# The second experts' shared expert: from fp32 products to products of split operands

## The chip, the cores and the metric

The kernel runs on one core of one Trainium2 chip. Its metric is the device time of one execution in microseconds; the median of three runs before the change is 1669.13 us (1666.88 to 1670.62). The engines are TensorE (PE), VectorE (DVE), ScalarE (ACT), GpSimd (POOL) and SyncE (SP), which issues most transfers.

## The reference

Two transformer blocks on 512 rows of 1024 columns. The first has a sparse attention beside a gated linear attention, then 32 experts, 2 for each row. The second has latent attention (MLA) beside attention with forget gates, and then these experts:

```python
h = rms_norm(x, g_ffn_norm) * (1 + scale_f) + shift_f
scores = sigmoid(h @ w_router)                 # 64 experts in 8 groups
choice = scores + b_router                     # 4 groups are kept, of these the 6 best experts
gate = scores[chosen] / sum(scores[chosen]) * 2.5
routed = sum over chosen e of gate_e * ((silu(h @ Wg[e]) * (h @ Wu[e])) @ Wd[e])
shared = (silu(h @ w_sh_gate) * (h @ w_sh_up)) @ w_sh_down     # 1024 -> 256 -> 1024, for all rows
x = x + gate_f * (shared + routed)
out = rms_norm(x, g_final)
```

All inputs and outputs are fp32. An fp32 product on PE is two passes, which the trace records as two instructions. The projections of both mixers avoid it: a matrix is split into a high part in fp32r (a format that PE takes in one pass) and the low part that is left, and three products (high by high, high by low, low by high) are summed in PSUM. This is `k.mm3` (lines 106 to 113).

## The kernel before, in words

Phases follow each other: mixer 1, 32 experts, mixer 2 (`phase_c`), 64 experts (`phase_d`, `rest_d`). Between phases, work overlaps where buffers and queues allow it. Rows are in four tiles (t = 0 to 3) of 128; `xres` is the residual in SBUF.

*Output projection wo* (`finish` in `phase_c`, L1805 to 1829). For each of two column groups of 512, four PSUM banks (one for each t) take eight steps of k, three products each: 96 matmuls of 128x512. The weights come by SP in four pieces of 256x512 (L130); ACT makes the high part wh (L136), DVE the low part wl (L137). DVE then multiplies a bank by the gate row gm (L1824, `wo<-wo,gmr`) and adds it to xres (L1825), and the bank is free for the second group. After the second group's add of tile t, `done(t)` starts the norm of that tile.

*Head of the second experts.* `head` and `logits` (L1886 to 1911): sum of squares on ACT, the root on DVE and ACT, then two steps on DVE: h = xres * rs * gs, and the shift, h + sh (L1903); h goes to DRAM (hD), is transposed on PE (xt, L1908), copied by ACT to hT, and multiplied with the router's weights (lg, L1911). `rest_d` starts with the sigmoid on ACT (L1931), adds the bias (L1933, `cv<-cv,br`), and follows a chain of small DVE steps that picks the experts up to Ab, the 0/1 matrix of choices (L1974). From Ab come, by small PE products and DVE steps, the counts cnt, the ranks of the experts (perm), the positions pos, posT and posR, the gates GT and Gr, and by bc and st the list ii of a unit's rows (L915).

*Shared expert.* Between these stand its products: gate and up g and u (L975) in fp32 with 128x256 outputs, hid = silu(g) * u (L977, L979), transposes (L986), y (L999), the scaling by the row gf on DVE into `ysh` (L1007), and the add to xres on POOL (L1993). Its weights sg (gate, up) and sd (down) come by `load_from` (L816 to 826).

*Units.* The routed experts run in 33 units of 128 rows, each of one or two experts' rows. For a unit, POOL gathers rows of hD by an indirect DMA into xg (L917), PE transposes them (L940), and multiplies with wg, wu (L975) and wd (L999); a product with a 0/1 matrix puts the result back to rows (L1053), and DVE adds it to xres.

*What sets the order.* A scheduler orders instructions on each engine by priorities (`high_priority`) when the program is built; an engine takes them in that order. Weights live in slots of 8 KB a partition, which `moe.slot` hands out from three pools (15, 2 and 1 slots) by the tables O1, then O2; a slot's next load waits for the last use of what it held. `rows`, `gmr` (the gate row gm, the norm's gain, later the router's weights), h4, hT4, sg and sd take slots as well. `moe.fetch(n)` loads the weights of units below n; F0 and F1 say up to which unit before and within the router. Experts from the fifth on are read through perm, by a register that SP loads (TENSOR_LOAD).

Of the kernel before, what the change touches and what calls it, by code (L numbers as in the profile page):

```python
# [7 lines left out]
F32 = mybir.dt.float32  # L8
F32R = mybir.dt.float32r
# [3 lines left out]
AF = mybir.ActivationFunctionType  # L13
# [5 lines left out]
S, D = 512, 1024  # L19
NT = 4  # L20
KD = 8
# [646 lines left out]
WS = (0, 1, 2, 2, 3, 3)  # L668
LAST = 2


# [76 lines left out]
class Moe:  # L748
# [33 lines left out]
    def slot(self, shape, dt, name, hold=False, after=None):  # L782


        t = self.W[next(self.order)].tile(shape, dt, tag="w8", name=name)
        if hold or after is not None:
            corner = t[:, 0, :1] if len(shape) == 3 else t[:, 0, 0, :1]
            with ExitStack() as c:
                if after is not None:
                    c.enter_context(self.k.tc.issue_after(after))  # L790
                self.k.nc.gpsimd.memset(corner, 0.0)
        return t

    def load(self, es, after=None, spread=(), free=0):
# [21 lines left out]
        return [(x[:2], x[2]) for x in g]  # L816

    def load_from(self, wg, wu, wd):

        nc = self.k.nc  # L820
        g = [self.slot([128, KD, 256], F32, "sg") for _ in range(2)]
        for t, w in zip(g, (wg, wu)):
            nc.sync.dma_start(t, w.rearrange("(p k) f -> p k f", p=128))
        d = self.slot([128, 2, D], F32, "sd")
        nc.sync.dma_start(d, wd.rearrange("(p j) n -> p j n", p=128))
        return g, d

# [229 lines left out]
    def run(self):  # L1057
        n = len(self.units)
        for u in range(2):
            self.pick(u)  # L1060
        self.prep(0)
        with self.k.tc.issue_after(self.indexed.ins):
            self.prep(1)
        if self.E == 32:
# [766 lines left out]

F0, F1 = 2, 3
NS = 9
RM = 15
RW = 1
O1 = [0] * 3 + [1] * 2 + [0] * 12
O2 = [0] * 3 + [1] * 2 + [2] + [0] * 12
LP = 300
RP = 300
FL = 0  # L1840
# [3 lines left out]
def phase_d(k, out):  # L1844
    nc, tc, I = k.nc, k.tc, k.I
    E = 64
    ctx = ExitStack()
# [12 lines left out]
    f = ctx.enter_context(tc.tile_pool(name="pd", bufs=1, reuse_waits="tile"))  # L1860
    moe_consts(k, f)
    gf = row(k, f, k.modD[5 * D:], "gf")
    moe.scale = gf
    perm = f.tile([1, E], I32, name="perm")
    rows_ = moe.slot([128, 2, D], F32, "rows")
    sh, gs = rows_[:, 0], rows_[:, 1]
# [12 lines left out]
    hTs = [hT4[t // 2][:, t % 2] for t in range(NT)]  # L1879
    shared = moe.load_from(I["w_sh_gate_2"][0], I["w_sh_up_2"][0], I["w_sh_down_2"][0])  # L1880
    moe.fetch(F0, 0)
    lbs = []
# [15 lines left out]
    def logits(t):  # L1898
# [3 lines left out]
        nc.vector.scalar_tensor_tensor(h, k.xres[:, t], rs, gs, op0=ALU.mult, op1=ALU.mult)  # L1902
        nc.vector.tensor_add(h, h, sh)  # L1903
        nc.scalar.dma_start(moe.hD[ts], h)
# [8 lines left out]
    def rest():  # L1913
        for t in range(NT - LL, NT):
            with tc.high_priority(LP):
                logits(t)
        moe.rooms()
        moe.work()
        rest_d(k, out, moe, lbs[0], br, f, perm, hTs, shared, ctx)
    return gm, head, rest  # L1920


def rest_d(k, out, moe, lb, br, f, perm, hTs, shared, ctx):
    nc, tc, I = k.nc, k.tc, k.I
# [60 lines left out]

    ws = [(128, shared)]
    hTx = moe.m.tile([128, NT, 2, 128], F32, tag="xT", name="hTx", bufs=1)
    for t in range(NT):
        moe.hidden(hTs[t], ws, None, k.pbank, hT=hTx[:, t])
    for t in range(NT):  # L1990
        def add(h, b):
            xs = k.xres[:, t, h * 512:(h + 1) * 512]
            nc.gpsimd.tensor_add(xs, xs, moe.scaled(h, b, moe.m.tile([128, 512], F32, tag="yl", name="ysh", bufs=2)))  # L1993
        moe.down(hTx[:, t], ws, add)
    moe.run()
# [72 lines left out]
```

## Time and profile before

| | us |
|---|---|
| median of 3 runs | 1669.13 |
| lowest, highest | 1666.88, 1670.62 |
| profiled execution | 1662.47 |
| its span | 1660.7 |
| PE busy in it | 1540.4 (93%) |
| DVE, ACT, POOL busy | 962.3, 542.9, 331.5 |

The profiled execution is 6.7 us under the median. A time in the trace is counted from the span's start. In a timeline row stand start, duration, engine, line, operation, output <- input, shape, the count of merged instructions, and in brackets the idle time of the engine ahead of it with what ended it. In a row of stages stand the busy time of each engine, PE's granted clock as a share of full speed, the DMA engines' mean share, and GB/s. A matmul's recorded duration is longer than its turn, since matmuls overlap; the distance of starts gives the rate.

### The profile page before, as it was taken

Reading aid. Unit: us, or ns where it says so; the run is one execution under the profiler, and the core shown is the slowest. Engines: PE = TensorE matmul, PEld = TensorE weight load, DVE = VectorE, ACT = ScalarE, POOL = GpSimd, SP = SyncE. Lnnn points to the kernel's source line nnn. Section 1 sums busy time; section 2 is a strip of 40 time slices with the busy share of each in tenths; the row PEclk is TensorE's granted clock in tenths of the full one; section 3 lists DMA queues with packets and bytes.
Section 4 is the critical chain, followed back from the end, with each engine's and each line's share of the span. In section 5 each row is a group of like instructions: output and inputs, shape, how many; then the busy total and the mean of one; then the engine's idle time right before and its main releaser. Section 6 shows DMA issues by size and latency. Waiting matters only on the chain.

```text
span 1660.7 us, 28614 instructions
## 1 busy us (share of the span) xinstructions
PE 1540.4 (93%) x10917; PEld 1037.9 (62%) x10917; DVE 962.3 (58%) x2188; ACT 542.9 (33%) x1100; POOL 331.5 (20%) x281
## 2 busy tenths in 40 slices
PE   5899999978998878899999998999999999999996
PEld 5665557765565547675657776865666665565663
DVE  3598636854564346547554635555665666666656
ACT  4534776331111125555552222301211211112112
POOL 2323541012111102230104442022101101111000
PEclk9999999988999998899999999999999999999998
DMA  6443326368999963233006836849999999999961
GB/s 189 148 164 112 114 80 242 126 216 323 418 416 416 419 256 105 73 93 103 26 1 191 263 111 233 308 184 366 375 414 388 398 416 417 423 419 420 420 287 64
DMA packets 104783, 420.78 MB, mean 253 GB/s; under 512 B 23508, under 2 KB 30138, under 8 KB 67268
## 3 DMA queue, kind: packets, MB, share of 16 engines
q1 hardware_dynamic: 82880, 388.20, 60.7%
q0 software_dynamic: 9968, 19.04, 3.2%
q10 hardware_dynamic: 11796, 11.68, 2.1%
q8 instruction: 87, 1.43, 0.3%
q14 instruction: 52, 0.43, 0.1%
HBM read 419.99 MB, written 9.21 MB: 258 GB/s over the span
## 4 chain that ended last, share of the span: by engine, by line
PE 49%; DVE 6%; DMA 4%; POOL 1%; ACT 1%; issue 1%; SPq 0%; DVEq 0%; ACTq 0%; POOLq 0%
PE g L975 8%; PE u L975 8%; PE sc L1053 7%; PE y L999 7%; PE qk L1690 2%; DMA mw<-in_w_mod_dram 2%; PE pt L110 2%; PE pt L108 2%; PE pt L109 2%; PE ob L1718 2%; PE xT L940 2%; PE pt L1710 1%; DVE macc L1402 1%; PE pr L109 1%; PE pr L108 1%
## 5 line engine op out<-in xcount | busy, mean ns | idle before, releaser
L137 POOL TENSOR_TENSOR wl<-w,wh 128x1024 fp32r<-128x1024 f32 (+4 forms) x68 | 156.6, 2305 | 360.4 <-ACT wh L136 336.9
L1054 DVE TENSOR_TENSOR xres<-xres,sc 128x512 f32<-128x512 f32 x368 | 224.3, 679 | 3.5 <-PE sc L1053 1.0
L975 PE MATMUL u<-wu,xT 128*32 128x256 f32 (+2 forms) x2240 | 175.3, 386 | 11.2 <-DMA wu<-in_w_exp_up_dram 9.4
L975 PE MATMUL g<-wg,xT 128*32 128x256 f32 (+2 forms) x2240 | 172.9, 382 | 3.1 <-DMA wg<-in_w_exp_gate_dram 3.1
L999 PE MATMUL y<-wd,hT 128*32 128x512 f32 (+2 forms) x1120 | 167.6, 596 | 0.0
L917 POOL DMA_INDIRECT xg<-hD,ii x46 | 46.1, 1002 | 597.1 <-issue 499.8
L981 DVE SCALAR_TENSOR_TENSOR hid<-u,gc,hid 128x256 f32<-128x256 f32 x46 | 22.2, 484 | 234.3 <-PE u L975 234.3
L975 PEld LDWEIGHTS g<-wg,xT 128*32 128x32 f32 (+2 forms) x2240 | 98.9, 118 | 89.6 <-issue 31.0
L1053 PE MATMUL sc<-yh,st 128*128 128x512 f32 x368 | 152.1, 416 | 0.0
L136 ACT ACTIVATE wh<-w 128x1024 fp32r<-128x1024 f32 (+4 forms) x88 | 89.9, 1021 | 185.1 <-PE pt L109 71.6
L975 PEld LDWEIGHTS u<-wu,xT 128*32 128x32 f32 (+2 forms) x2240 | 104.3, 120 | 73.2 <-DMA wu<-in_w_exp_up_dram 12.2
L1053 PE MATMUL sc<-yl,st 128*128 128x512 f32 x368 | 144.4, 395 | 0.1
L989 ACT ACTIVATE hT<-hT 128x256 f32<-128x256 f32 x46 | 17.7, 385 | 298.8 <-PE hT L986 298.8
L116 ACT ACTIVATE yh<-y 128x512 fp32r<-128x512 f32 x92 | 55.0, 597 | 163.3 <-DVE y L1007 129.4
L108 PE MATMUL pr<-wh,xh 128*128 128x512 f32 (+2 forms) x256 | 102.1, 403 | 5.9 <-ACT wh L136 5.4
L109 PE MATMUL pr<-wl,xh 128*128 128x512 f32 (+2 forms) x256 | 101.8, 399 | 5.9 <-POOL wl L137 5.9
L999 PEld LDWEIGHTS y<-wd,hT 128*32 128x32 f32 (+2 forms) x1120 | 46.6, 118 | 90.7 <-issue 88.6
L117 DVE TENSOR_TENSOR yl<-y,yh 128x512 fp32r<-128x512 f32 x92 | 63.6, 691 | 67.1 <-ACT yh L116 66.7
L110 PE MATMUL pr<-wh,xl 128*128 128x512 f32 (+2 forms) x256 | 100.3, 396 | 0.2 <-DVE xl L117 0.2
L110 PE MATMUL pt<-xh,wl 128*128 128x512 f32 x224 | 89.2, 398 | 1.8 <-POOL wl L137 1.7
L108 PE MATMUL pt<-xh,wh 128*128 128x512 f32 x224 | 89.8, 401 | 0.1
L109 PE MATMUL pt<-xl,wh 128*128 128x512 f32 x224 | 88.6, 396 | 0.0
(540 smaller groups left out, 2797.7 us busy)
## 6 DMA issues: line engine op xcount, KB each, us to landing
wg<-in_w_exp_gate_dram SPq DMA_DIRECT2D x96, 1024.0 KB, 12.7
wu<-in_w_exp_up_dram SPq DMA_DIRECT2D x96, 1024.0 KB, 12.4
wd<-in_w_exp_down_dram SPq DMA_DIRECT2D x96, 1024.0 KB, 11.5
w<-in_w_in_dram SPq DMA_DIRECT2D x52, 512.0 KB, 3.8
mw<-in_w_mod_dram SPq DMA_DIRECT2D x32, 512.0 KB, 6.0
mw<-in_w_mod_dram SPq DMA_DIRECT2D x8, 1024.0 KB, 6.0
w<-in_w_out_dram SPq DMA_DIRECT2D x16, 512.0 KB, 4.9
brs<-brd ACTq DMA_DIRECT2D x1, 2560.0 KB
```

The lines of the kernel that those rows point to most:

```text
L108: nc.tensor.matmul(out, lhsT=lh, rhs=rh, start=first, stop=False)
L109: nc.tensor.matmul(out, lhsT=lh, rhs=rl, start=False, stop=False)
L110: nc.tensor.matmul(out, lhsT=ll, rhs=rh, start=False, stop=last)
L116: hi = nc.scalar.activation(dh, src, AF.Copy)
L117: lo = nc.vector.tensor_sub(dl, src, dh.bitcast(F32))
L136: nc.scalar.activation(wh[:, :, :c], w[:, :, :c], AF.Copy)
L137: (eng or nc.gpsimd).tensor_sub(wl[:, :, :c], w[:, :, :c], wh[:, :, :c].bitcast(F32))
L917: self.gathered = nc.gpsimd.indirect_dma_start(out=x, out_offset=None, in_=src, in_offset=bass.IndirectOffsetOnAxis(ap=ii[:, :1], axis=0), ...
L975: nc.tensor.matmul(b[sl], lhsT=xT[:, kk, sl], rhs=g[h][:, kk], start=kk == 0, stop=kk == KD - 1)
L999: nc.tensor.matmul(b[sl], lhsT=hT[:, j, sl], rhs=d[:, j, h * 512:(h + 1) * 512], start=j == 0, stop=j == 1)
L1053: nc.tensor.matmul(b, lhsT=st[:, ts], rhs=y[h][i], start=i == 0, stop=i == 1)
L1054: nc.vector.tensor_add(self.acc[:, t, hs], self.acc[:, t, hs], b)
```

## The change

The shared expert is computed from split operands. Its gate and up weights stand side by side in two tiles sgu of 512 columns, which are split into sgh (ACT) and sgl (DVE); sd is multiplied by gf once and split into sdh and sdl; hT is split into hh (ACT) and hl (DVE), the latter behind the last tile's shift (`shifted[-1]`). `gu(t)` makes gate and up of a tile in one bank by 24 products of 128x512, `turned(t)` the hidden rows, their transposes and their split into mh and mid; y then comes scaled, and DVE adds it from PSUM to xres. The tables O1 and O2, F0 and the priorities of the first units' preparation are new as well.

```diff
@@ -667,6 +667,7 @@
 OB = [1] * 4 + [0] * 7 + [1] + [2] * 2 + [3] * 3
 WS = (0, 1, 2, 2, 3, 3)
 LAST = 2
+RUN = {32: 0, 64: 400}
 
 
 SEQ = "mfmtmtmfmtmtmmtmmtmtmmtmmtmtmtm"
@@ -788,7 +789,7 @@
             with ExitStack() as c:
                 if after is not None:
                     c.enter_context(self.k.tc.issue_after(after))
-                self.k.nc.gpsimd.memset(corner, 0.0)
+                self.k.nc.gpsimd.memset(corner.bitcast(F32) if dt == F32R else corner, 0.0)
         return t
 
     def load(self, es, after=None, spread=(), free=0):
@@ -814,16 +815,6 @@
             g[i][2] = self.slot([128, 2, D], F32, "wd", after=after)
             self.last.append(get(g[i][2], sl(self.wd, e)))
         return [(x[:2], x[2]) for x in g]
-
-    def load_from(self, wg, wu, wd):
-
-        nc = self.k.nc
-        g = [self.slot([128, KD, 256], F32, "sg") for _ in range(2)]
-        for t, w in zip(g, (wg, wu)):
-            nc.sync.dma_start(t, w.rearrange("(p k) f -> p k f", p=128))
-        d = self.slot([128, 2, D], F32, "sd")
-        nc.sync.dma_start(d, wd.rearrange("(p j) n -> p j n", p=128))
-        return g, d
 
     def rank(self, m, perm):
 
@@ -1056,11 +1047,12 @@
 
     def run(self):
         n = len(self.units)
-        for u in range(2):
-            self.pick(u)
-        self.prep(0)
-        with self.k.tc.issue_after(self.indexed.ins):
-            self.prep(1)
+        with self.k.tc.high_priority(RUN[self.E]):
+            for u in range(2):
+                self.pick(u)
+            self.prep(0)
+            with self.k.tc.issue_after(self.indexed.ins):
+                self.prep(1)
         if self.E == 32:
             self.fetch(3, after=self.gathered.ins, free=NF)
         self.take(0)
@@ -1829,13 +1821,14 @@
     return finish
 
 
-F0, F1 = 2, 3
+F0, F1 = 1, 3
 NS = 9
 RM = 15
 RW = 1
-O1 = [0] * 3 + [1] * 2 + [0] * 12
-O2 = [0] * 3 + [1] * 2 + [2] + [0] * 12
+O1 = [0] * 18 + [1] * 2 + [0] * 6
+O2 = [0, 2] + [0] * 5 + [1] * 2 + [0] * 9
 LP = 300
+SH = 600
 RP = 300
 FL = 0
 FP = 300
@@ -1862,6 +1855,13 @@
     gf = row(k, f, k.modD[5 * D:], "gf")
     moe.scale = gf
     perm = f.tile([1, E], I32, name="perm")
+    sgu = [moe.slot([128, 4, 512], F32, "sgu") for _ in range(2)]
+    for q in range(2):
+        for c, n in enumerate(("w_sh_gate_2", "w_sh_up_2")):
+            nc.sync.dma_start(sgu[q][:, :, 256 * c:256 * c + 256],
+                              I[n][0].rearrange("(p k) f -> p k f", p=128)[:, 4 * q:4 * q + 4])
+    sd = moe.slot([128, 2, D], F32, "sd")
+    nc.sync.dma_start(sd, I["w_sh_down_2"][0].rearrange("(j p) n -> p j n", p=128))
     rows_ = moe.slot([128, 2, D], F32, "rows")
     sh, gs = rows_[:, 0], rows_[:, 1]
     nc.scalar.dma_start(rows_, k.modD[3 * D:5 * D].rearrange("(o d) -> o d", o=2)[None].to_broadcast([128, 2, D]))
@@ -1877,7 +1877,24 @@
     h4 = [moe.slot([128, 2, D], F32, "h4", True) for _ in range(2)]
     hT4 = [moe.slot([128, 2, KD, 128], F32, "hT4", True) for _ in range(2)]
     hTs = [hT4[t // 2][:, t % 2] for t in range(NT)]
-    shared = moe.load_from(I["w_sh_gate_2"][0], I["w_sh_up_2"][0], I["w_sh_down_2"][0])
+
+    def part(n, shape=(128, 4, 512), hold=False):
+        return moe.slot(list(shape), F32R, n, hold)
+    rows4 = (128, 2, KD, 128)
+    hs = [[part(n, rows4, True)] for n in ("hh", "hl")]
+    sgu2 = [[part(n) for n in ("sgh", "sgl")] for _ in range(2)]
+
+    for w, (wh, wl) in zip(sgu, sgu2):
+        nc.scalar.activation(wh, w, AF.Copy)
+        nc.vector.tensor_sub(wl, w, wh.bitcast(F32))
+    sdh = part("sdh", (128, 2, D))
+    sdl = part("sdl", (128, 2, D), True)
+    mid = part("mid", hold=True)
+    nc.vector.tensor_mul(sd, sd, gf[:, None, :].to_broadcast([128, 2, D]))
+    nc.scalar.activation(sdh, sd, AF.Copy)
+    down, shifted = (sd, sdh, sdl), []
+    for c, n in zip(hs, ("hh", "hl")):
+        c.append(part(n, rows4, True))
     moe.fetch(F0, 0)
     lbs = []
 
@@ -1900,7 +1917,7 @@
         ts = slice(t * 128, (t + 1) * 128)
         h, hT = h4[t // 2][:, t % 2], hTs[t]
         nc.vector.scalar_tensor_tensor(h, k.xres[:, t], rs, gs, op0=ALU.mult, op1=ALU.mult)
-        nc.vector.tensor_add(h, h, sh)
+        shifted.append(nc.vector.tensor_add(h, h, sh).ins)
         nc.scalar.dma_start(moe.hD[ts], h)
         for c in range(2):
             b = k.bank("xt")
@@ -1914,13 +1931,23 @@
         for t in range(NT - LL, NT):
             with tc.high_priority(LP):
                 logits(t)
+        with tc.high_priority(LP):
+            for t in range(NT):
+                hh, hl = [x[t // 2][:, t % 2] for x in hs]
+                nc.scalar.activation(hh, hTs[t], AF.Copy)
+                with tc.issue_after(shifted[-1]):
+                    nc.vector.tensor_sub(hl, hTs[t], hh.bitcast(F32))
+            sd, sdh, sdl = down
+            with tc.issue_after(shifted[-1]):
+                nc.vector.tensor_sub(sdl, sd, sdh.bitcast(F32))
         moe.rooms()
         moe.work()
-        rest_d(k, out, moe, lbs[0], br, f, perm, hTs, shared, ctx)
+        moe.fetch(2, 0)
+        rest_d(k, out, moe, lbs[0], br, f, perm, hTs, hs, (sgu2, sdh, sdl, mid), ctx)
     return gm, head, rest
 
 
-def rest_d(k, out, moe, lb, br, f, perm, hTs, shared, ctx):
+def rest_d(k, out, moe, lb, br, f, perm, hTs, hs, shared, ctx):
     nc, tc, I = k.nc, k.tc, k.I
     E = 64
     p = Carve(moe)
@@ -1983,15 +2010,39 @@
     moe.ranked(Gt, p, f)
 
 
-    ws = [(128, shared)]
-    hTx = moe.m.tile([128, NT, 2, 128], F32, tag="xT", name="hTx", bufs=1)
+    sgu, sdh, sdl, mid = shared
+    mh = moe.m.tile([128, NT, 2, 128], F32R, tag="xT", name="mh", bufs=1)
+    ml = mid[:, 2:].rearrange("p a (c j s) -> p (a c) j s", c=2, j=2)
+    hid = hTs[NT - 1].rearrange("p (t a) n -> p t (a n)", t=NT)
+    gus = {}
+
+    def gu(t):
+        hh, hl = [x[t // 2][:, t % 2] for x in hs]
+        b = gus[t] = k.pbank("gu")
+        for kk in range(KD):
+            wh, wl = [w[:, kk % 4] for w in sgu[kk // 4]]
+            k.mm3(b, hh[:, kk], hl[:, kk], wh, wl, kk == 0, kk == KD - 1)
+        nc.scalar.activation(hid[:, t], b[:, :256], AF.Silu)
+
+    def turned(t):
+        with tc.high_priority(SH):
+            nc.vector.tensor_mul(hid[:, t], gus[t][:, 256:], hid[:, t])
+            b = k.pbank("hT")
+            for j in range(2):
+                nc.tensor.transpose(b[:, j * 128:(j + 1) * 128], hid[:, t, j * 128:(j + 1) * 128], k.ident)
+            k.split(mh[:, t], ml[:, t], b[:, :256].rearrange("p (j s) -> p j s", j=2))
+    gu(0)
+    for t in range(1, NT):
+        gu(t)
+        turned(t - 1)
+    turned(NT - 1)
     for t in range(NT):
-        moe.hidden(hTs[t], ws, None, k.pbank, hT=hTx[:, t])
-    for t in range(NT):
-        def add(h, b):
-            xs = k.xres[:, t, h * 512:(h + 1) * 512]
-            nc.gpsimd.tensor_add(xs, xs, moe.scaled(h, b, moe.m.tile([128, 512], F32, tag="yl", name="ysh", bufs=2)))
-        moe.down(hTx[:, t], ws, add)
+        for h in range(2):
+            cs = slice(512 * h, 512 * h + 512)
+            b = k.pbank("y")
+            for j in range(2):
+                k.mm3(b, mh[:, t, j], ml[:, t, j], sdh[:, j, cs], sdl[:, j, cs], j == 0, j == 1)
+            nc.vector.tensor_add(k.xres[:, t, cs], k.xres[:, t, cs], b)
     moe.run()
     gl = moe.slot([128, 2, D], F32, "gl")[:, 0]
     nc.scalar.dma_start(gl, I["g_final_2"][None, :].to_broadcast([128, D]))
```

The order of DVE's instructions in wo, before (rows is the norm's gain with its scale, wl the low part of a piece of the weights, L1825 the add that frees a bank):

```order
L137 TENSOR_TENSOR wl<-w,wh 128x1024
L1871 SCALAR_TENSOR_TENSOR rows<-rows,gmr 128x1024
L137 TENSOR_TENSOR wl<-w,wh 128x1024
L1824 TENSOR_TENSOR wo<-wo,gmr 128x512
L1825 TENSOR_TENSOR xres<-xres,wo 128x512
L1824 TENSOR_TENSOR wo<-wo,gmr 128x512
L1825 TENSOR_TENSOR xres<-xres,wo 128x512
```

And after, where L1816 and L1817 are the former L1824 and L1825, L1893 the product of sd with gf, and L1889 the split of sgu:

```order
L137 TENSOR_TENSOR wl<-w,wh 128x1024 x2
L1893 TENSOR_TENSOR sd<-sd,gf 128x2048
L1871 SCALAR_TENSOR_TENSOR rows<-rows,gmr 128x1024
L1816 TENSOR_TENSOR wo<-wo,gmr 128x512
L1889 TENSOR_TENSOR sgl<-sgu,sgh 128x2048
L137 TENSOR_TENSOR wl<-w,wh 128x1024 x2
L1889 TENSOR_TENSOR sgl<-sgu,sgh 128x2048
L1817 TENSOR_TENSOR xres<-xres,wo 128x512
```

Four operations of 2048 or 1024 columns now stand between the first product with gm and the first add to xres, and the product of sd with gf stands ahead of rows.

PE's order around the first list of rows, before (bc leads to ii, y is the shared expert's output, xT the transposes of unit 0's gathered rows):

```order
L986 MATMUL hT<-ident,hid 128x128 x2
L975 MATMUL g<-sg,hT_9355 128x256 x2
L861 MATMUL Gr<-cv 128x64 x4
L865 MATMUL ce<-cv 64x2
L975 MATMUL g<-sg,hT_9355 128x256 x6
L975 MATMUL u<-sg,hT_9355 128x256 x8
L905 MATMUL bc<-posT,sel 128x512 x2
L986 MATMUL hT<-ident,hid 128x128 x2
L999 MATMUL y<-sd,hTx 128x512 x16
L940 MATMUL xT<-ident,xg_9792 128x128 x8
```

And after:

```order
L108 MATMUL y<-sdh,mh 128x512
L109 MATMUL y<-sdl,mh 128x512
L889 MATMUL posR<-cv 64x512
L848 MATMUL GT<-ident,cv 64x128 x4
L110 MATMUL y<-sdh,mid 128x512
L108 MATMUL y<-sdh,mh 128x512
L109 MATMUL y<-sdl,mh 128x512
L110 MATMUL y<-sdh,mid 128x512
L108 MATMUL y<-sdh,mh 128x512
L852 MATMUL Gr<-cv 128x64 x4
L856 MATMUL ce<-cv 64x2
L896 MATMUL bc<-posT,sel 128x512 x2
```

The 16 products of g and u ahead of bc are gone, and seven of y stand there; 15 of gu stand further ahead, between the first use of Ab and posT.

SP's order of loads, before:

```order
L825 DMA sd<-in_w_sh_down_dram 128x2048
L804 DMA wg<-in_w_exp_gate_dram 128x2048
L130 DMA w<-in_w_out_dram 128x2x512 x2
L804 DMA wg<-in_w_exp_gate_dram 128x2048
L804 DMA wu<-in_w_exp_up_dram 128x2048 x2
L804 DMA wd<-in_w_exp_down_dram 128x2048 x2
L804 DMA wg<-in_w_exp_gate_dram 128x2048 x2
L804 DMA wu<-in_w_exp_up_dram 128x2048 x2
L804 DMA wd<-in_w_exp_down_dram 128x2048 x2
L1852 TENSOR_LOAD perm
L1852 ISA x2
```

And after:

```order
L1864 DMA sd<-in_w_sh_down_dram 128x2x1024
L130 DMA w<-in_w_out_dram 128x2x512 x3
L805 DMA wg<-in_w_exp_gate_dram 128x2048 x3
L805 DMA wu<-in_w_exp_up_dram 128x2048 x2
L805 DMA wd<-in_w_exp_down_dram 128x2048 x2
L1845 TENSOR_LOAD perm
L1845 ISA x2
L1845 TENSOR_LOAD perm
L1845 ISA x2
L805 DMA wg<-in_w_exp_gate_dram 128x2048
L805 DMA wu<-in_w_exp_up_dram 128x2048 x2
L805 DMA wd<-in_w_exp_down_dram 128x2048
```

The first two reads of perm stand behind unit 0's six loads and one of unit 1, and ahead of the rest of unit 1's; before, they stood behind unit 1's loads.

## Rows read from the trace of the kernel before

**Rows 1.** The page, busy time by engine.

```profile
PE 1540.4 (93%) x10917; PEld 1037.9 (62%) x10917; DVE 962.3 (58%) x2188; ACT 542.9 (33%) x1100; POOL 331.5 (20%) x281
```

**Rows 2.** Stages: us, busy time and count by engine, PE clock, DMA share, GB/s.

```profile
1010.00:1020.00 10.00, 8.44 (x37) 6.50 (x36) 1.94 (x3) 2.26 (x3) 0.00 (x0) 1.00 0.91 346
1020.00:1030.00 10.00, 7.00 (x20) 5.60 (x21) 5.07 (x6) 0.00 (x0) 0.00 (x0) 0.66 0.96 358
1110.00:1120.00 10.00, 10.00 (x26) 4.50 (x25) 4.21 (x9) 0.00 (x0) 9.31 (x9) 1.00 0.44 156
1300.00:1400.00 100.00, 100.00 (x977) 61.02 (x973) 63.57 (x136) 18.44 (x37) 11.94 (x12) 1.00 1.01 417
```

**Rows 3.** PE's waits from 1127 to 1600: us, times, longest.

```profile
PE hT L986 <- DVE hid L981: 0.7, 1, 0.7
```

**Rows 4.** PE's timeline, shared expert's end: start, us, instruction, [idle].

```profile
1101.56 3.62 PE L975 MATMUL u<-sg,hT 128*128 128x256 f32 x16
...
1106.11 13.90 PE L999 MATMUL y<-sd,hTx 128*128 128x512 f32 x32
1119.84 1.05 PE L940 MATMUL xT<-ident,xg 128*128 128x128 f32 x8
...
1121.36 1.91 PE L975 MATMUL g<-wg,xT 128*32 128x256 f32 x26
```

**Rows 5.** PE's timeline in wo.

```profile
1023.00 0.79 PE L109 MATMUL wo<-wl,xh 128*128 128x512 f32 x1 [4.55 <-DVE wl L137]
...
1028.22 0.39 PE L110 MATMUL wo<-wh,xl 128*128 128x512 f32 x1
...
1038.72 0.39 PE L108 MATMUL wo<-wh,xh 128*128 128x512 f32 x1
...
1039.40 0.39 PE L108 MATMUL wo<-wh,xh 128*128 128x512 f32 x1
...
1056.41 0.39 PE L110 MATMUL wo<-wh,xl 128*128 128x512 f32 x1
```

**Rows 6.** DVE's timeline in wo and at the last shift.

```profile
1020.58 1.22 DVE L1871 SCALAR_TENSOR_TENSOR rows<-rows,gmr 128x1024 f32<-128x1024 f32 x1 [7.79 <-DMA gmr<-in_g_ffn_norm_dram]
...
1067.15 1.23 DVE L1903 TENSOR_TENSOR h<-h,rows 128x1024 f32<-128x1024 f32 x1
```

**Rows 7.** DVE's timeline in the router.

```profile
1076.77 0.42 DVE L979 TENSOR_TENSOR hid<-u,hid 128x256 f32<-128x256 f32 x1 [8.34 <-PE u L975]
1077.11 0.41 DVE L1933 TENSOR_TENSOR cv<-cv,br 128x256 f32<-128x256 f32 x1
...
1088.19 0.42 DVE L1974 TENSOR_TENSOR Ab<-cv 128x256 bf16<-128x256 f32 x1
...
1107.32 0.14 DVE L915 TENSOR_SCALAR ii<-ix 128x1 int32<-128x1 f32 x1
```

**Rows 8.** Stages in the first experts' norm, columns as in 2.

```profile
618.00:627.00 9.00, 0.38 (x3) 0.03 (x1) 5.56 (x27) 4.42 (x12) 0.51 (x1) 0.72 0.12 27
627.00:633.00 6.00, 4.99 (x19) 3.91 (x19) 6.00 (x13) 4.39 (x13) 2.52 (x2) 0.50 0.45 112
633.00:639.00 6.00, 6.00 (x19) 5.46 (x20) 2.61 (x10) 1.78 (x7) 2.27 (x1) 0.50 0.55 145
```

**Rows 9.** ACT's timeline before the router.

```profile
1070.42 1.08 ACT L1909 ACTIVATE hT<-xt 128x512 f32<-128x512 f32 x2
1071.52 1.28 ACT L1931 ACT_TABLE_LOAD   x1
1075.35 0.38 ACT L1931 ACTIVATE cv<-lg 128x256 f32<-128x256 f32 x1 [2.55 <-PE lg L1911]
```

**Rows 10.** POOL's timeline, first gather.

```profile
1108.26 1.09 POOL L917 DMA_INDIRECT xg<-hD,ii  x1 [49.10 <-DVE st L908]
```

**Rows 11.** Tile xg, first gather, then those at 1136 and 1152.

```profile
DMA to landing us min/median/max: 5.5/5.5/5.5
...
DMA to landing us min/median/max: 8.8/9.2/9.6
```

## The prediction, made before the changed kernel ran

> **What bounds the kernel now.** I read the page first: TensorE is busy 93% of the span [rows 1], so a gain has to come from its holes, its clock or its work. Then I cut the span by stage [rows 2]. From 1300 on PE is busy 100% of the time at full clock while DMA moves 417 GB/s at share 1.01: there both are full, and from 1127 to 1600 PE waits 0.7 us in all [rows 3]. The change touches nothing there, except what it starts with. What it touches lies between 1010 and about 1121, where the output projection of the second mixer (wo), the second experts' norm, router and shared expert stand, and where PE has holes: 7.00 of 10 us from 1020, at a mean clock of 0.66 [rows 2]. The end of the kernel moves by as much as unit 0's first product moves, at 1121.36 [rows 4], if the weights keep ahead.
>
> PE's and DVE's timelines are read next, for which wait ends last. In wo PE stops 4.55 us for wl [rows 5]. DVE stands still 7.79 us for gmr ahead of that wl [rows 6], because an operation on rows is ahead of it in DVE's order. After the stop twelve products take the 5.2 us from 1023.00 to 1028.22, 0.43 each against 0.23 later: half clock, about 2.5 us more. In the head, DVE waits 8.34 us for PE's u ahead of the router's first step at 1077.11 [rows 7]. So two things bound it in turn: PE's shared-expert products, which stand in the way of the router's small matmuls, and DVE, which takes the router's chain in its order. Last comes y, which holds PE until 1119.84 [rows 4].
>
> **The change, part by part.** Sums are made against the profiled execution of 1662.47 us (span 1660.7, 1.8 around it). The median of three runs is 1669.13, 6.7 above; I take the difference over to the median.
>
> PE's work: gate and up were 128 records of fp32 at 3.47 us for 16 (1101.56 to the end of the row at 1105.18, less 0.15 by which the last record outlasts its turn), so 0.217 each and 27.8 us; y is 13.90 us [rows 4]. In place of them come 96 products of 512 columns and 48 more for y. wo has products of that very form, at (1039.40 - 1038.72)/3 = 0.227 us [rows 5]: 21.8 + 10.9 = 32.7. PE has 9.0 us less to do. That isn't the gain, as PE isn't all that stands on the path. I walk the path in five steps.
>
> A, wo. The wait of 4.55 us goes: in the new order rows stands behind wl. But sd times gf and rows, then the first wo times gm, two sgl subtractions and two wl stand ahead of the first xres add, and the second column group's first product needs that bank. The transfers in front: 0.5 MB of w_out on its way at 1010, 2.1 of sgu, 0.5 of w_out, 1.05 of sd, 1.05 of rows, 0.5 of gmr and 0.5 of gm are 6.2 MB. At 346 to 358 GB/s [rows 2] the last lands at about 1010 + 6.2/0.35 = 1027.7. Rows and gmr also leave later, since ACT's queue now has them behind a fourth wh. From there DVE in order: wo 0.7, sgl 2.4 (twice the 1.22 of 1024 columns [rows 6]), two wl 2.4, sgl 2.4, xres 0.7: about 1036.4. The first group ends now near 1033.8 (1056.8 less 21.8 for the second and 1.2 for short waits in it); without the stop of 4.55 and the 2.5 it ends near 1026.7, so PE is idle some 9.7 us. The second group is 96 products, 21.8, and I add 2.5 for the half clock as after the stop of 4.55 us. Its end is about 1060.7, against 1056.8 [rows 5]. The last shift moves from 1068.38 [rows 6] to 1072.1: **+3.7**. Bounds: +1 if transfers run at the 417 GB/s of 1300 [rows 2] and the clock holds, +7 if sd lands 3 us later and the clock is slow as after 618 [rows 8].
>
> B, last shift to the router's first step (cv plus br), before 8.73 (1068.38 to 1077.11). DVE no longer stands at hid waiting for u. ACT's way is: transposes 0.6, three hT copies of 0.54, two hh of 1.08 (as hh has 1024 columns, two of hT's 512), the table 1.28, the sigmoid 0.38 [rows 9], about 6.2 with hand-overs. The four hl subtractions (4.8 us on DVE) lie beside it; their cover is 1.4 us wide. **-2.5** (0 to -3.5).
>
> C, router's first step to Ab, before 11.5 [rows 7]. sdl is now inside, 2.4, and three hid and two mid of 0.34 to 0.35 where one hid was: 2.4 + 4 x 0.35 and 0.1 for hand-over, **+3.9** (+2.5 to +5, the upper if DVE waits for a hT bank or for gu).
>
> D, Ab to ii, before 18.85. In it PE took 26 products of the shared expert, 52 records at 0.217, 11.3 us, in order between the router's small matmuls. Now 15 of gu and 7 of y stand there at 0.227, 5.0. DVE gets about 2.2 more (a mid, xres adds of the wo form), of which I put 1.5 beside PE's work, since the y products ahead of bc don't wait for DVE. 18.85 - 11.3 + 5.0 + 0.7 = 13.2: **-5.6** (-3 to -8).
>
> E, ii to unit 0's first product, before 13.9: PE was in y until 1119.84, and the gather, issued 0.8 after ii, landed 5.5 later and was hidden [rows 4, 10, 11]. Now y would be done near 1114, and the gather isn't hidden. SP's order has the read of perm ahead of most of unit 1's weights, and the slots of sgh, hh and hl come free with the last gu, so 7 or 8 MiB start right before the gather. The gathers that ran beside a full stream took 8.8 and 9.6 [rows 11]; I take 9.2, and 0.8 + 9.2 + 1.5 (transposes, copy) = 11.5: **-2.4**. Bounds: landing 5.5 gives -6, if y then isn't late; 12 gives +0.4.
>
> POOL's eight xres adds go to DVE as PSUM adds; POOL's gather issues have nothing ahead of them then.
>
> Sum: 3.7 - 2.5 + 3.9 - 5.6 - 2.4 = **-2.9**: unit 0 starts near 1118.4. Units and tail follow unchanged, since PE waits for no weight there [rows 3]. 1669.13 - 2.9 = 1666.2 us.
>
> **The rivals.** *The gather is short.* If its landing is 5.5 as in the first row of [rows 11] and not 9.2, PE's y is last and T0 near 1114 to 1115.4: -6, or -9 if wo also costs only +1. For it: DMA's share was 0.44 in the old head, from 1110 [rows 2]. Against it: the released slots. 1662.
>
> *The clock (slower than before).* PE stops 9.7 us in wo, and the new head has only four gu products between the transposes before the last shift, where 16 fp32 records of g stood before; PE is then idle while ACT and DVE make hh and hl. The rows at 618 show the price [rows 8]: after a stretch in which PE is busy 0.38 of 9 us the granted clock is 0.50 from 627 to 639, the lower of its levels, and PE is busy 4.99 and 6.00 us in it: 11 us of work at half speed, so 5.5 lost. In the second wo group that is 5.5 for the 2.5 that I took, +3.0. In the head the same would cost 0 to 5.5, by what of it lies beside DVE; I take 3.3, the middle and a little. -2.9 + 3.0 + 3.3 = +3.4, 1672.5 (1669.2 to 1674.7). The sign turns where clock costs 2.9 more than mine. Against it: after 1023 the clock came back by 1028 [rows 5]. [...]
>
> *The stream bounds it.* 1300 to 1400 runs at 417 GB/s with share 1.01 [rows 2]; if unit 1's and 2's weights, now released later, miss their time, units start late and the gain is given back: 0, or a little above, 1669. Against it: PE's only wait from 1127 to 1600 is for DVE [rows 3].
>
> *The change saves nothing on PE.* If the split products ran at 0.434 instead of 0.227 PE would have 30 us more. wo's rows exclude it.
>
> **How the numbers follow.** Forecast, 1663 to 1669.5, chance 0.5. Short gather, 0.2. Clock, 0.2. Stream, 0.1. 0.2% is 3.3 us, which is about what a measurement of this kernel can tell from no change; the forecast lies on that bound at 1666.2, so I count half of it less a little as faster and the rest as same. Faster: 0.2 from the short gather and 0.22 from the forecast; slower: 0.16 from the clock and 0.03 from the stream; same: the rest, 0.39. The range reaches from the short gather with a cheap wo (1669.1 - 9 = 1660, and 1 for scatter) to the clock rival's upper half (1674.5).
>
> **What would show it.** A: idle on PE ahead of the second wo group, ended by DVE's xres; a DVE wait for sd; last shift near 1072. B: the router's first step about 6 after it, with no wait for PE's u. C: 15 us to Ab. D: ii near 1107. E: the first transposes of xg waiting for DMA and landing around 9 us. The clock: granted below 1 beyond 1045, or between 1060 and 1080. I'd be wrong if PE's second group starts before 1030 (gm and sd early), if the first gather lands under 6 us, or if PE waits for weights after unit 0. The units themselves should take as long as now.

## The result, and the profile after

The changed kernel takes 1681.67 us (median of 6 runs, 1680.08 to 1683.55), the kernel before 1669.66 beside it: a ratio of 1.0075, interval 1.006 to 1.009, so 12 us slower. Forecast were 1666.2. The profiled execution of after has a span of 1681.8 us, 21.1 above that of before.

That difference is more than the runs', and part of it isn't the change's: the 30 units from unit 2 to unit 32 take 474.5 us in the trace of before and 478.8 in that of after, though their code is the same. A kernel with the changed kernel's stream and split (the sixth below) has 474.4. So 4.3 us belong to that execution and not to the change, and steps are compared from one marker to the next:

| from, to | before | after | forecast |
|---|---|---|---|
| first wo product to last shift | 62.4 | 68.8 | +3.7 |
| last shift to the router's first step | 10.0 | 8.5 | -2.5 |
| router's first step to Ab | 11.1 | 16.2 | +3.9 |
| Ab to ii | 19.1 | 13.9 | -5.6 |
| ii to unit 0's first product | 14.0 | 12.2 | -2.4 |
| unit 0's to unit 1's first product | 14.9 | 26.8 | 0 |

All are starts of instructions, so the second row differs a little from a count from the shift's end. The first five sum to +2.9, against -2.9; the sixth, which the forecast left unchanged, is +11.9. Unit 1 so starts 14.8 us later behind wo's first product, while the medians differ by 12.0; the 2.8 us between the two counts stay open. Unit 1's first product in the trace of before:

```profile
1136.25 3.03 PE L975 MATMUL g<-wg,xT 128*64 128x256 f32 x26
```

Stages of after, with the columns of [rows 2]:

```profile
1030.00:1040.00 10.00, 1.78 (x4) 1.24 (x5) 10.00 (x11) 3.80 (x3) 0.20 (x2) 0.68 0.39 131
1110.00:1120.00 10.00, 10.00 (x49) 8.17 (x48) 6.73 (x21) 0.00 (x0) 1.09 (x1) 1.00 1.01 421
1120.00:1130.00 10.00, 6.42 (x43) 3.39 (x41) 0.00 (x0) 1.08 (x2) 1.89 (x2) 0.83 1.03 423
1130.00:1140.00 10.00, 1.91 (x18) 1.09 (x18) 4.92 (x21) 0.00 (x0) 2.14 (x3) 0.63 0.67 277
1300.00:1400.00 100.00, 100.00 (x956) 63.93 (x949) 61.26 (x131) 18.30 (x36) 11.97 (x12) 1.00 0.99 404
```

PE is busy 1.78 of 10 us from 1030 and 1.91 of 10 from 1130; from 1300 on it is full, as before. From 1110 to 1130 DMA runs at 421 and 423 GB/s where it was at 156 [rows 2]. PE's three longest waits from 1000 on (us in total, times, longest):

```profile
PE wo L108 <- DVE xres L1817: 9.9, 1, 9.9
PE ov L1106 <- DVE rw L1110: 8.9, 1, 8.9
PE xT L931 <- DMA xg<-hD,ii: 2.8, 1, 2.8
```

Before, there was one stop, of 4.55 us in wo [rows 5], and from 1127 on PE waited 0.7 us in all [rows 3]. Now there are one of 9.9 in wo, one of 8.9 inside unit 0 and one of 2.8 for the first gather. DVE's timeline answers to [rows 6, 7]:

```profile
1026.78 2.29 DVE L1893 TENSOR_TENSOR sd<-sd,gf 128x2048 f32<-128x2048 f32 x1 [7.17 <-DMA sd<-in_w_sh_down_dram]
1028.99 1.22 DVE L1871 SCALAR_TENSOR_TENSOR rows<-rows,gmr 128x1024 f32<-128x1024 f32 x1
...
1030.72 2.28 DVE L1889 TENSOR_TENSOR sgl<-sgu,sgh 128x2048 fp32r<-128x2048 f32 x1
1032.92 2.35 DVE L137 TENSOR_TENSOR wl<-w,wh 128x1024 fp32r<-128x1024 f32 x2
1035.19 2.28 DVE L1889 TENSOR_TENSOR sgl<-sgu,sgh 128x2048 fp32r<-128x2048 f32 x1
1037.39 0.68 DVE L1817 TENSOR_TENSOR xres<-xres,wo 128x512 f32<-128x512 f32 x1
...
1074.90 1.23 DVE L1920 TENSOR_TENSOR h<-h,rows 128x1024 f32<-128x1024 f32 x1
...
1083.38 0.43 DVE L1960 TENSOR_TENSOR cv<-cv,br 128x256 f32<-128x256 f32 x1 [0.73 <-ACT cv L1958]
...
1090.95 0.43 DVE L117 TENSOR_TENSOR mid<-hT,mh 128x256 fp32r<-128x256 f32 x1 [1.53 <-ACT mh L116]
...
1099.54 0.42 DVE L2001 TENSOR_TENSOR Ab<-cv 128x256 bf16<-128x256 f32 x1
...
1113.46 0.15 DVE L906 TENSOR_SCALAR ii<-ix 128x1 int32<-128x1 f32 x1
```

It waits 7.17 us for sd, then does sd, rows and, after one product with gm, the splits of sgu and two wl, before it adds the first bank to xres at 1037.39. PE's second column group starts with that, and at half clock, as its records show, 0.63 us at first and 0.39 later (twelve products from 1038.22 to 1043.50, at a granted clock of 0.50):

```profile
1038.22 0.77 PE L108 MATMUL wo<-wh,xh 128*128 128x512 f32 x1 [9.88 <-DVE xres L1817]
```

In the router's part the row of 1090.95 shows a wait that wasn't counted, 1.53 us for ACT's mh, in front of a step of the chain. Ab starts at 1099.54, ii at 1113.46. Unit 0 in PE's timeline, which answers to [rows 4]:

```profile
1124.03 1.13 PE L931 MATMUL xT<-ident,xg 128*128 128x128 f32 x8 [2.81 <-DMA xg<-hD,ii]
...
1125.63 3.60 PE L966 MATMUL g<-wg,xT 128*32 128x256 f32 x26
1138.10 0.56 PE L1106 MATMUL ov<-two,ex 64*128 64x4 f32 x2 [8.86 <-DVE rw L1110]
...
1152.43 3.67 PE L966 MATMUL g<-wg,xT 128*64 128x256 f32 x32
```

PE waits 2.81 us for the gathered rows, starts g at 1125.63, does a part of it at half clock (0.50 granted from 1125.70 to 1129.00, with PE busy all of the time, and 0.50 from 1132.60 to 1142.60), and stops for 8.86 us; unit 1 starts at 1152.43. What stands behind the stop is in the chain of waits between 1108 and 1142, in order of time (start, us, what):

```profile
1111.28 15.78 DMA gD<-cv
...
1127.81 6.14 DMA gg<-gD,ii
...
1133.97 0.15 DVE gc L941
...
1134.47 1.88 DVE xres L2045 x3
...
1137.02 0.07 DVE rw L1108
```

The gate rows of all experts, gD, leave for DRAM at 1111.28 and take 15.78 us. Only then can POOL gather unit 0's gates from them (gg, 6.14 us). DVE waits for gg with gc, and behind gc in its order stand three adds to xres, a list and rw, a step of the table for rows over an expert's place. PE's next instruction is ov, which waits for rw. Nothing in unit 0 needs gc until its hid, which in the trace of before starts at 1130.57, 9.2 us behind the unit's first product. In the trace of before the same write:

```profile
1099.23 0.38 ACTq L863 DMA_DIRECT2D gD<-cv  x1
1101.76 0.38 ACT L977 ACTIVATE hid<-g 128x256 f32<-128x256 f32 x1 [4.50 <-DMA gD<-cv]
```

It left at 1099.23, and ACT, which waited for it, went on at 1101.76: at most 2.5 us. What is different in after is on SP's queue:

```profile
1105.50 0.33 SPq L805 DMA_DIRECT2D wg<-in_w_exp_gate_dram  x1
1105.88 0.90 SPq L805 DMA_DIRECT2D wu<-in_w_exp_up_dram  x2
1106.88 1.62 SPq L805 DMA_DIRECT2D wd<-in_w_exp_down_dram  x2
1108.76 0.94 SPq L805 DMA_DIRECT2D wg<-in_w_exp_gate_dram  x2
1110.30 11.05 SPq L805 DMA_DIRECT2D wu<-in_w_exp_up_dram  x2
```

From 1105.50 to 1111 eight loads of 1 MiB leave (the second of the last row only at 1121), the ones that the first reads of perm and the free slots let go together. At 421 GB/s 8.4 MB take 20 us, to about 1125 (an estimate), and gD, issued behind them, lands at 1127. It doesn't stand still until they are done: packet by packet, the trace has the write's 528 packets (512 of 256 bytes, 16 of 4) spread from 1114.95 to 1126.65, among packets of 8 KB of the weights. In the trace of before the same 528 run from 1100.59 to 1101.42.

### The profile page after: what moved, and what is told of

It is laid out like the page before. It is cut to its first block, busy times and chain, and to the rows that moved or that the text cites. A ratio compares the mean times of both kernels' runs of the same rounds, so it can differ in the third digit from the quotient of the medians.

```text
span 1681.8 us, 28602 instructions
## 1 busy us (share of the span) xinstructions
PE 1546.4 (92%) x10901; PEld 1059.1 (63%) x10901; DVE 975.1 (58%) x2200; ACT 551.3 (33%) x1106; POOL 323.4 (19%) x279
## 4 chain that ended last, share of the span: by engine, by line
PE 51%; DMA 4%; DVE 4%; ACT 1%; POOL 1%; issue 1%; SPq 0%; DVEq 0%; ACTq 0%; POOLq 0%
PE sc L1044 7%; PE g L966 7%; PE y L990 7%; PE u L966 7%; PE pt L110 2%; PE pt L108 2%; PE pt L109 2%; PE qk L1682 2%; PE ob L1710 2%; PE xT L931 2%; DMA mw<-in_w_mod_dram 1%; PE pt L1702 1%; DMA gD<-cv 1%; POOL wl L137 1%; DVE macc L1394 1%
## 5 line engine op out<-in xcount | busy, mean ns | idle before, releaser
L966 PE MATMUL u<-wu,xT 128*32 128x256 f32 (+2 forms) x2240 | 180.5, 389 | 10.7 <-DMA wu<-in_w_exp_up_dram 8.9
L966 PE MATMUL g<-wg,xT 128*32 128x256 f32 (+2 forms) x2240 | 181.1, 389 | 1.4 <-DMA wg<-in_w_exp_gate_dram 1.4
L966 PEld LDWEIGHTS g<-wg,xT 128*32 128x32 f32 (+2 forms) x2240 | 105.1, 120 | 87.6 <-issue 35.9
L966 PEld LDWEIGHTS u<-wu,xT 128*32 128x32 f32 (+2 forms) x2240 | 120.3, 121 | 60.5 <-DMA wu<-in_w_exp_up_dram 11.3
L980 ACT ACTIVATE hT<-hT 128x256 f32<-128x256 f32 x46 | 17.7, 385 | 299.9 <-PE hT L977 299.9
```

The source lines that it names most:

```text
L966: nc.tensor.matmul(b[sl], lhsT=xT[:, kk, sl], rhs=g[h][:, kk], start=kk == 0, stop=kk == KD - 1)
```

## The experiments

Each was timed in rounds with the kernel before on the same chip; the first four stood beside 1669.18 us on one chip, the last four beside 1663.64 on another, so ratios are what compares. In the code, ` ...` marks lines left out. 0.1% is 1.67 us.

**Unit 0's gate copies later (first attempt).**

```diff
-        self.take(0)
+        if self.E == 64:
+            self.xT[0] = self.turn(self.xg[0][0])
+        else:
+            self.take(0)
         self.pick(2)
         self.prep(2)
         self.table()
         self.pick(3)
+        if self.E == 64:
+            self.gates(0)
```

> The only edit is on VectorE: the three copies of unit 0's gates (gc from gg) stand behind the overflow table's steps instead of ahead of them. Theory G (the gate rows gD reach DRAM late, behind the released weights, so that gg lands late, and VectorE, which takes its work in order, holds the table's rw back, for which TensorE stops 8.9 us inside unit 0): the stop on ov goes, TensorE goes on through unit 0's g and u and waits only for hid, some 2 us; unit 1 starts 6 to 9 us earlier; 1673 to 1676 us, against 1681.7 of the changed kernel. Rival C (the loss is TensorE's half clock after its stop in wo, and the stop in unit 0 only covers a later wait of the same length): same as the changed kernel, 1680 to 1683. Rival S (unit 1's weights are what is late): 1680 to 1683, with the wait moved to unit 1's g.

1681.06 us, ratio 1.0081 (1.0056 to 1.0107): no change. But it isn't the test that was meant. The copies came to stand behind `prep(2)`, which fills the same buffer, so they took unit 2's gates and left out unit 0's, and waited for that later gather as well. The stop on ov went, and in its place stands

```profile
PE hT L977 <- DVE hid L972: 6.8, 1, 6.8
```

so it decides nothing; it was done again as the fifth.

**The stream held.**

```diff
-        if self.E == 32:
-            self.fetch(3, after=self.gathered.ins, free=NF)
+        self.fetch(3, after=self.gathered.ins, free=NF if self.E == 32 else 0)
 ...
-        moe.fetch(2, 0)
 ...
-    moe.positions(Ab, p, perm, lambda: moe.fetch(F1))
+    moe.positions(Ab, p, perm, None)
```

> The weights of units 1 and 2 are loaded behind the issue of the first two units' gathers, by a GpSimd memset in each slot; the order on TensorE, VectorE and ScalarE is the changed kernel's. Theory G: gD lands some 3 us after its issue instead of 16, the first xg in 5 instead of 9.5 us, the stop of 8.9 us on ov goes, and unit 1 starts 12 to 15 us earlier: 1666 to 1670 us. Rival C: 1680 to 1683. Rival S (the stream bounds the first units): unit 1's weights come later by some 10 us, TensorE waits for them, 1682 to 1692.

1665.61 us, ratio 0.998 (0.9963 to 0.9997): 16 us below the changed kernel, and a little below the one before. The order of PE, DVE and ACT is the changed kernel's. In its timeline gD, the first xg and gg:

```profile
1109.52 0.38 ACTq L854 DMA_DIRECT2D gD<-cv  x1
...
1112.64 1.09 POOL L908 DMA_INDIRECT xg<-hD,ii  x1 [49.34 <-DVE st L899]
...
1114.04 1.03 POOL L908 DMA_INDIRECT gg<-gD,ii  x1 [0.30 <-issue]
```

gg is issued right behind xg, and doesn't wait for gD. What is left of PE's waits (the two longest; each of the others is 0.7 us or less):

```profile
PE wo L108 <- DVE xres L1816: 10.5, 1, 10.5
PE lg L1927 <- ACT hT L1925: 3.3, 1, 3.3
```

The stop in wo is as long as before, those for ov and xg are gone. Unit 0 starts 9.1 us after ii (12.2 in after) and takes 14.2 (26.8), at a granted clock of 1.00 (0.75). The held weights of unit 1 are nowhere waited for.

**wo clear.** The split of the weights becomes a function that runs behind the last evacuation of the first column group:

```diff
+    def between(prior):
+        with tc.issue_after(prior):
+            for w, (wh, wl) in zip(sgu, sgu2):
+                nc.scalar.activation(wh, w, AF.Copy)
+                nc.vector.tensor_sub(wl, w, wh.bitcast(F32))
+            nc.vector.tensor_mul(sd, sd, gf[:, None, :].to_broadcast([128, 2, D]))
 ...
+            if not g:
+                between(added.ins)
```

> The two sgl subtractions and the product of sd with gf stand behind the four evacuations of wo's first column group instead of ahead of the first. Theory A (the 9.9 us stop ahead of the second column group and its half clock are these 7 us of VectorE and the wait for sd): the stop falls to 0 to 2 us, the half clock behind it goes, the last shift comes 8 to 11 us earlier, unit 0 too, and the stop in unit 0 stays: 1671 to 1674 us. Rival: the gate row gm lands as late as sd, so that the stop only falls to 5 us or more: 1677 to 1679. Rival E (what is won here is lost at the gather, since the release of the stream moves along): same as the changed kernel within 3 us.

1676.85 us, ratio 1.0044 (1.0025 to 1.0063): 5 us better, less than was expected. The stop falls from 9.88 to 3.29, and the half clock behind it, which was expected to go, stays for twelve products (0.50 granted). The timeline row, and the stage behind it (columns as in [rows 2]):

```profile
1029.97 0.77 PE L108 MATMUL wo<-wh,xh 128*128 128x512 f32 x1 [3.29 <-DVE xres L1818]
1029.97:1035.87 5.90, 5.62 (x12) 4.06 (x13) 5.90 (x8) 1.52 (x1) 0.00 (x0) 0.50 0.51 165
```

DVE's first product there waits for the gate row gm, until 1027.94: that is the first rival, though with a stop shorter than its 5 us.

First wo product to last shift takes 62.7 us, 6.1 less than in after and about as long as before the change (62.4): of these wo takes 50.5 (after 56.6, before 51.7 with its own stop), and the norm behind it 12.2 as in after. Unit 0 starts 6.1 earlier behind wo's first product and takes 26.9, as in after; the two costs are apart.

**The priority of the first units' preparation undone** (`RUN = {32: 0, 64: 0}`).

> The priority of the first units' preparation goes back to 0: VectorE adds all of y ahead of the first list of rows, so the first gather is issued some 7 us later, near 1121. Theory G: gD has nearly landed by then, gg follows the first xg at once, the stop in unit 0 goes, but unit 0 starts 6 us later: 1677 to 1681 us. Rival (the early list is what makes the kernel faster): unit 0 and unit 1 both start 7 us later, 1687 to 1690.

1681.51 us, ratio 1.0067 (1.0041 to 1.0092): the changed kernel's time. ii moves from 13.9 to 23.5 us behind Ab, unit 0 from 119.5 to 127.3 behind wo's first product, and unit 0 takes 15.6 instead of 26.8. The wait only changes its place:

```profile
PE xT L931 <- DMA xg<-hD,ii: 11.9, 1, 11.9
```

The norm is short again: 10.75 us from the last wo product to the last shift, as before the change, against 12.19 in after. There, the earlier preparation puts four casts into DVE's order within the norm, in one block:

```profile
1063.42 2.05 DVE L918 CAST sel<-ident 128x96 fp32r<-128x96 f32 x4
```

**The gate copies behind the table**, ahead of the gather that refills their buffer.

```diff
-        self.take(0)
-        self.pick(2)
-        self.prep(2)
-        self.table()
+        if self.E == 64:
+            self.xT[0] = self.turn(self.xg[0][0])
+            self.pick(2)
+            self.table()
+            with self.k.tc.issue_after(self.tabled.ins):
+                self.gates(0)
+            self.prep(2)
 ...
```

> As the first run meant it: unit 0's gate copies stand behind the table's last step on VectorE, but ahead of the gather that fills their buffer with unit 2's gates; the weights are released as in the changed kernel, and gD lands as late. Theory G (the stop in unit 0 is VectorE's order: gc, which waits for gg, ahead of rw, which TensorE waits for): gg lands near 1134, and g and u of unit 0 last until about 1135, so TensorE has no stop on ov and waits 0 to 1 us for hid; unit 1 starts 10 to 12 us earlier, 1669 to 1673 us. Rival (gg lands later than 1140, as the gathers of the table and of unit 2 now collide with it): TensorE waits 5 to 8 us for hid, 1677 to 1682.

1668.75 us beside 1663.64, ratio 1.0041 (1.0025 to 1.0056), 0.34% or some 6 us better than the changed kernel; 10 to 12 were expected. In DVE's timeline rw now comes first, and gc still waits for a late gg:

```profile
1124.34 0.16 DVE L1116 COPY rw<-ov 128x4 f32<-128x4 f32 x1 [3.40 <-PE ov L1114]
...
1133.14 0.47 DVE L941 COPY gc<-gg 64x1 f32<-64x1 f32 x3 [3.81 <-DMA gg<-gD,ii]
```

PE has no stop on ov, and unit 0 takes 17.7 us. So DVE's order turned the late write into PE's stop. What keeps unit 0 from the 14.2 us of the held stream is the clock: PE stood 2.64 us for the first gather just ahead of it, and the clock granted in unit 0 is 0.81, against 1.00 there. Unit 0 as a stage in after, here, and with the stream held:

```profile
1125.63:1152.43 26.80, 17.23 (x179) 7.86 (x178) 8.48 (x33) 2.72 (x6) 8.07 (x8) 0.75 0.78 308
1124.29:1141.97 17.68, 16.97 (x180) 7.83 (x179) 7.01 (x30) 2.89 (x6) 8.12 (x8) 0.81 0.99 408
1120.83:1135.03 14.20, 13.52 (x180) 7.28 (x179) 6.05 (x27) 2.71 (x6) 4.03 (x4) 1.00 1.00 402
```

PE is busy 17.0 us here where the same work took 13.5 at a clock of 1.00.

**gD on another queue.**

```diff
-        nc.scalar.dma_start(self.gD.rearrange("(t p) e -> p t e", p=128), G)
+        (nc.scalar if E == 32 else nc.gpsimd).dma_start(self.gD.rearrange("(t p) e -> p t e", p=128), G)
```

> Only the queue of gD's write changes: GpSimd issues it ahead of the first gather, instead of ScalarE. Theory Q (what holds gD back for 16 us is the queue that it is on, behind or beside the hardware queue of the weights, since xg, which GpSimd issued 3 us later, landed 4 us earlier): gD lands in 5 to 10 us, near 1121, gg near 1130, the stop on ov falls from 8.9 to 2 to 5 us, the first xg 1 us later; 1673 to 1678 us. Rival B (any small write waits for the 8 MB that are on their way): gD lands near 1127 again, 1680 to 1684.

1665.89 us, ratio 1.0009 (0.9999 to 1.002): 11 us better than the changed kernel, by one instruction's queue, with the stream as early as there. POOL's timeline, and the write's time to landing:

```profile
1111.97 0.82 POOL L854 DMA_DIRECT2D gD<-cv  x1 [45.98 <-DVE cv L853]
1114.84 1.09 POOL L908 DMA_INDIRECT xg<-hD,ii  x1 [2.04 <-DVE st L899]
1118.66 1.03 POOL L908 DMA_INDIRECT gg<-gD,ii  x1 [2.73 <-DVE two L1096]
```

```profile
DMA to landing us min/median/max: 5.9/5.9/5.9
```

5.9 us instead of 15.8; POOL can issue gg at 1118.66, gc has it at 1125.25, and unit 0 takes 15.6. The write's time is within what was expected, the gain is larger: the stop goes whole. But the edit changes more than the queue. Packets, MB and share in after from 1111 to 1127 (ACT's queue), and here from 1112 to 1118 (POOL's):

```profile
q10 hardware_dynamic: 528, 0.13, 3.7%
q0 software_dynamic: 48, 0.13, 5.5%
```

The same 128 KB, 512 packets of 256 bytes there, are 32 of 4 KB here (16 of 4 bytes are with either), and they run from 1116.10 to 1117.55. Whether the queue or the size of the packets makes the difference isn't told apart by this run.

**wo clear and the stream held, together.**

> The second and the third run together: the split of the weights behind wo's first evacuations, and the weights of units 1 and 2 behind the first gathers. Theory: the two costs are independent, wo 5 to 8 us and the gates' chain 16 us, so 1681.7 - 16 - 5 to 8 = 1657.5 to 1660.5 us, 9 to 12 below the kernel before. Rival (with unit 0 earlier, the held weights of unit 1 come too late): TensorE waits for wg or wu in unit 1, 1663 to 1668.

1655.7 us, ratio 0.9956 (0.994 to 0.9972): some 7 us below the kernel before, where 9 to 12 were expected, and, by the ratios (1.0075 and 0.9956), some 20 below the changed one; within the intervals the two costs of 5 and 16 us add up. PE's two longest waits from 1000 on:

```profile
PE wo L108 <- DVE xres L1817: 3.4, 1, 3.4
PE lg L1934 <- ACT hT L1932: 2.5, 1, 2.5
```

Unit 0 starts 110.3 us behind wo's first product, against 116.7 before, and takes 14.1.

**And sdl behind Ab.**

```diff
-            with tc.issue_after(shifted[-1]):
-                nc.vector.tensor_sub(sdl, sd, sdh.bitcast(F32))
 ...
+    with tc.issue_after(summed.ins):        # summed: the add that makes Ab
+        low()                               # the same subtraction
```

> As the run before, with the subtraction sdl behind Ab on VectorE instead of within the router's chain. Theory C-term (sdl's 2.3 us lie on the path from the router's first step to Ab): Ab 2 us earlier, and so the first list, unit 0 and the end, unless TensorE's gu or y end later: 1 to 2.5 us below the run before. Rival (TensorE's products set the end of the head once the chain is shorter, and y waits for sdl): no change, within 1 us of the run before.

1656.26 us, ratio 0.996 (0.9944 to 0.9976), the same as the run before. Ab comes 2.1 us earlier behind wo's first product (85.2 instead of 87.3), and ii 2.4 later behind Ab (16.3, 13.9): what the chain gained it gave back behind it.

## Why the prediction was wrong

*The step that failed* stands in the sum: "Units and tail follow unchanged, since PE waits for no weight there." It asked of unit 0 only for weights. Unit 0 also needs its gates, by a write to DRAM, a gather from it and copies on DVE, and this chain of transfers was counted nowhere. Behind E it says that "POOL's gather issues have nothing ahead of them then": gg had the write of gD ahead of it. Held stream (unit 0 takes 14.2), other queue (15.6) and other order on DVE (17.7) each take most of the 11.9 us away, by three different links of one chain, so this cause is shown. Of the 11.9 us some 8 are PE standing still and some 4 its work at a lower clock (17.2 us busy at 0.75 for 13.5 at 1.00). It is worth more than the whole loss: with the stream held the time falls by 16 us, of which 3 are the first gather.

*The release of the stream* was foreseen in E, with its reason (perm read early, slots free with the last gu), and its price for the first gather was right: 9.5 us in the trace, 9.2 in the forecast. What wasn't asked is what else leaves in those 20 us. The rival on the stream looked for late weights alone, and PE never waited for one.

*A* had the mechanism and the stop right (9.7 forecast, 9.88 measured, a granted clock of 0.50 behind it), but the step is +6.4, not +3.7; its own terms, an end at 1060.7 for 1056.8, give +3.9. Of the 2.7 missed 1.4 lie behind wo: from the last wo product to the last shift it took 10.75 us and takes 12.19, which the forecast left unchanged. These are the four casts of the first units' preparation: with its priority undone the norm takes 10.75 again. The rest is small differences in wo. That the stop fits so well is partly luck: the sum hid DVE's products of sd and rows, 3.5 us, within the transfers, which it let end at 1027.7; in the trace sd was there at 1026.78, and both products came behind it. The run with wo clear shows what the work on DVE is worth: wo alone falls from 56.6 to 50.5.

*B* -1.5 (forecast -2.5), *C* +5.1 (+3.9; the wait of 1.53 for mh wasn't in it), *D* -5.2 (-5.6) and *E* -1.9 (-2.4) were near. With the stream held E is -4.9, near the short gather's case (-6).

*The clock*, the rival that would have been slower, is seen: 0.68 from 1030, 0.78 from 1070, 0.83 and 0.63 from 1120 and 1130. These are means over 10 us; the traces of before and after record it at 1.00 or at 0.50 and at nothing between. Behind the stop in wo it cost what the forecast had taken, twelve products at 0.50, and not the 3.0 more that the rival asked; in the head B and C came out 1.0 and 1.2 us worse than forecast, and how much of that is clock isn't shown. Its largest price is where the rival didn't look, in unit 0: 3.7 us in after (0.75), by the stage rows of the fifth run, and still 3.5 (0.81) where only the wait for the first gather, 2.64 us, stands ahead of it (the fifth run itself). Where that wait is gone as well, with the stream held, unit 0 has 1.00.

*PE's saving*: the head's work did shrink (the shared expert's gate, up and y are 160 records of fp32 in the trace of before, two for each product, and 144 in that of after, one for each product, those of y 0.233 us apart), and with both costs away the kernel is 7 us faster than before, near the 9.0 of the forecast's first sum; as PE's work isn't all of the path, that they meet may be chance.

## What to carry to other kernels

When a change lets loads go earlier or together, list every other transfer that leaves while they are on their way, small writes above all, and walk each to who waits for it. DVE took its work in order and made the wait of one copy the wait of everything behind it (rw behind gc, 8.86 us of PE; with rw first, none): put a copy that waits for a transfer behind the steps that others wait for. A step forecast as "unchanged" needs its own inputs looked up, all of them.

## What was not expected of the hardware

The same write of 128 KB took at most 2.5 us in the kernel before, 15.8 behind eight loads of 1 MiB on ACT's queue, and 5.9 on POOL's queue with those loads on their way; a gather that POOL issued 3 us behind the slow write landed 3 us ahead of it (1114.40 and 9.5 us, against 1127). So the load alone doesn't decide; the sixth run changed the queue and, with it, the packets, from 512 of 256 bytes to 32 of 4 KB. The packets speak for their size: from the write's first packet to its last, 11.7 us in the trace of after, 538 packets of 8 KB start beside its 528. The median packet of 8 KB takes 0.309 us there, one of the write 0.018. If the 528 are shared evenly by the 16 engines of the page, 33 each, and each stands behind one packet of 8 KB, the write takes 10 us. That is an estimate; a write with larger packets on ACT's queue, which would decide it, was not run.

Of the same code, 30 units took 474.5 us in one execution and 478.8 in another, with PE busy throughout and its clock granted in full from 1300 to 1400 in both. The traces of the first four experiments, taken on one chip, have 476.5 to 478.9, those of the last four, on another, 474.4 in all; the kernel before is 5.5 us quicker there, too. So it goes with the chip or the hour rather than with the edits; why, stays open.
